# The last value block of two FFN parts: both halves joined in one step, at a higher priority

## The chip, the cores and the metric

One core of one Trainium2 chip. The metric is device time in microseconds, the median over runs. TensorE (PE in the profile) multiplies matrices into PSUM; VectorE (DVE) and ScalarE (ACT) work element by element; GpSimd (POOL) here issues the loads that add to what is already in the buffer; SyncE (SP) issues most other transfers. Each engine takes its instructions in the order that the program's scheduler wrote.

## The reference

A decoder layer over 256 tokens of width 2048. It ends with a gated FFN behind a causal convolution, and the change lies there (`h` is the residual stream):

```python
def conv_gated_ffn(hn, w_up, conv_w, conv_b, w_down):
    up = causal_dwconv(hn @ w_up, conv_w, conv_b)      # D_FF = 5632, 3 taps
    gate, val = jnp.split(up, 2, axis=-1)
    return (jax.nn.silu(gate) * val) @ w_down
...
hn = rmsnorm(h, norm_ffn_w[l])
h = h + conv_gated_ffn(hn, ffn_w_up[l], ffn_conv_w[l], ffn_conv_b[l], ffn_w_down[l])
```

Ahead of it stand two token mixers with eight wide projections and a cross-attention over 256 memory tokens. All arithmetic is float32.

## The kernel before

**Products in two pieces.** A float32 operand is split into a rounded part and the rest: `hi` and `lo` for weights (L286 on ScalarE copies `raw` into `hi`, L287 on VectorE takes `lo` = `raw` - `hi`), and one tile `s` with both pieces for activations (`split_pair`, L555 and L556). A product is then hi x hi and lo x hi (L362 and L363, in `upper_n`) and hi x lo (L369, in `lower_n`).

**The weight stream.** Weights come in pieces of 4 x 128 rows by 512 columns, 1 MB each, in one written order. `prefetch` takes the next unit of that order: it loads the piece into one of six `raw` buffers (L265 on SP; L267 on GpSimd where a piece is added onto a loaded one), and splits it into one of three `hi` and three `lo` buffers. It runs two units ahead of TensorE. Between units, `later(n, fn)` runs `fn` after n + 1 more units have been issued; this is how steps of one stage are written in among the products of the next.

**Pairs of columns.** Where two blocks of 512 columns are multiplied together (`pair_products`), eleven units replace the eight plain ones, with seven products of sums of blocks on one part of the rows. Their order and what happens to the weights:

```python
PAIR_UNITS = [
    ("q1", "A", ("new", 0, 0)), ("p0", None, (1, 8)), ("q3", "B", ("new", 1, 1)),
    ("p1", None, (0, 8)), ("q5", "A", ("add", 0, 1)), ("q2", "C", ("new", 1, 0)),
    ("q6", "A", ("sum",)), ("p2", None, (1, 12)), ("q7", "B", ("add", 0, 1)),
    ("q4", "A", ("sum",)), ("p3", None, (0, 12)),
]
```

A, B and C are `raw` buffers that stay in use. A piece is added to A for q5 and to B for q7 by the loads of L267. L294 adds B to A behind q5's split, for q6. L292 adds C to A behind q6's split, for q4. The units p0 to p3 are plain row products: p2 and p3 use the activation tiles 6 and 7, the seven q units only sums and tiles 0 to 3, p0 and p1 tiles 4 and 5. A q unit has 8 products of L362 and L363 and 4 of L369, a p unit 16 and 8. When units are done, their sums are added to the residual rows on VectorE (L427).

**The FFN.** It is cut into three parts of 4, 4 and 3 blocks of 512 hidden columns. In each part, for each block: the gate columns, then the value columns, are multiplied (`gemm_n`); the result leaves PSUM as two 16-bit planes (L757), is turned by two DMA transposes (L1205) and joined again in two halves by `join_planes` (L763 on ScalarE, two copies a half) and scaled (L1271 on VectorE). Then come the convolution (`conv`: L1281 on ScalarE, four steps of L1283 on VectorE a half), the gating and the split (`hidden`: L1354 on ScalarE, L1355 and L1356 on VectorE, then L555 and L556). The tiles that come out, two a block, are the activations of the down product, which follows as two pairs of columns in the first two parts.

`up(c0, b, at, then)` does this for one block; `at` says after how many units each half is joined. All blocks have (1, 2), the last value block of the first two parts (2, 4): its halves give tiles 6 and 7, are joined while the first pair of down columns already runs, and are first used in its eighth unit, p2. The third part has no pairs and another path there.

**What sets the order.** The program is scheduled instruction by instruction: on each engine the ready one with the lowest number goes first, and the numbers follow the order of writing. `tc.high_priority(URGENT)`, with `URGENT` 5, moves what is written inside it forward.

Of the kernel before, what the change touches and what calls it, by code (L numbers as in the profile page):

```python
# [14 lines left out]
ALU = mybir.AluOpType  # L15
# [11 lines left out]
FF = 5632  # L27
# [8 lines left out]
URGENT = 5  # L36
# [118 lines left out]
def hybrid_layer(  # L155
# [16 lines left out]
    act, dve, pe, pool, sp = nc.scalar, nc.vector, nc.tensor, nc.gpsimd, nc.sync  # L172
# [17 lines left out]
    def big(shape, dt=F32, s="b"):  # L190
        return bp.tile(shape, dt, tag="big", name=nm(s))

    def tmp(s="t"):
        return tp.tile([P, 2, S], F32, tag="tmp", name=nm(s))
# [109 lines left out]
    def later(n, fn):  # L304

        pending.append((step[0] + n + 1, fn))
# [21 lines left out]
    def gemm_t(w, row, st, nk, col):  # L328

        accs = [acc(), acc()]  # L330
        first = gemms[0] == 0
        phase = 0
        for k0, parts in chunks(nk, w, row, col):
            last = k0 + KC >= nk
            tiles = [(kk, j) for j in range(2) for kk in range(KC)]
            if first and k0 == 0:
                runs = [[(t, pr, kk, j) for t in (0, 1)] for pr in range(2) for kk in range(KC) for j in range(2)]
            elif last:
                runs = [[(t, pr, kk, j) for kk, j in tiles] for pr in range(2) for t in (1 - pr, pr)]
            else:  # L340
                runs = [[(t, pr, kk, j) for pr in range(2) for kk, j in tiles] for t in (phase, 1 - phase)]
                phase = 1 - phase
            for i, run in enumerate(runs):
                for t, pr, kk, j in run:
                    k = k0 + kk
                    sx = st[k // 2][:, k % 2, :]
                    part = parts[kk // KH][t][:, kk % KH, (2 * pr + j) * P : (2 * pr + j + 1) * P]
                    a = accs[pr][:, j, :]
                    if t == 1:
                        a, sx = a[:, S:BW], sx[:, 0:S]  # L350
                    pe.matmul(  # L351
                        a, part, sx, start=k == 0 and t == 0, stop=k == nk - 1 and t == 0, skip_group_check=True
                    )
                if i + 1 == len(runs) // 2 and not last:
                    st[(k0 + KC) // 2 + 1]
        return accs
# [14 lines left out]
    def gemm_n(w, row, st, nk, col):  # L371

        a = acc()
        for k0, parts in chunks(nk, w, row, col):
            ops = [
                [halves(st[(k0 + k) // 2], (k0 + k) % 2, slice(tt * P, (tt + 1) * P)) for k in range(KC)]
                for tt in range(2)
            ]
            for tt in range(2):
                upper_n(a[:, tt, :], ops[tt], parts, k0 == 0)  # L380
            for tt in range(2):
                lower_n(a[:, tt, :], ops[tt], parts, k0 + KC >= nk)
        return a
# [288 lines left out]
    rsb2 = rsb[:, None, :].to_broadcast([P, 2, S])  # L672

    def scaled(a, s):
        z = joined(a, s)
        dve.tensor_tensor(out=z, in0=z, in1=rsb2, op=ALU.mult)
        return z
# [72 lines left out]
    def words(t):  # L750

        return t.bitcast(U16).rearrange("p t (w two) -> p t w two", two=2)
# [6 lines left out]
    def join_planes(d, pr):  # L759

        t = tmp("jp")
        for i in range(2):
            ins = act.copy(words(t)[:, :, :, 1 - i], d[:, i, 2 * pr : 2 * pr + 2, :])  # L763
            if i == 0:
                tc.keep_in_program_order(ins)
        return t
# [115 lines left out]
    for g in range(2):  # L882
        dec = big([P, 4, S], s="dec")
        vs, turned = [], []
        for b, o in enumerate((O_Q, O_K)):
            a = qjoin if g == b == 0 else [joined(t, "q") for t in gemm_t("w_in", 0, xs, NT, o + g * BW)]
            if b == 0:
                sp.dma_start(
                    out=dec,
# [295 lines left out]
    def row_planes(o):  # L1185

        t = big([P, 2, 2, BW], U16, s="rp")
        planes(t, o)
        return t
# [11 lines left out]
    def turn_planes(rows):  # L1201

        d = big([P, 2, KC, S], U16, s="d")
        for tt in range(2):
            sp.dma_start_transpose(  # L1205
                out=d.rearrange("p a c s -> p (a c) s")[:, :, tt * P : (tt + 1) * P],
                in_=rows[:, tt].rearrange("p a w -> p (a w)"),
            )
        return d
# [51 lines left out]
    def up(c0, b, at, then):  # L1261

        if at is None:
            for pr, a in enumerate(gemm_t("ffn_w_up", 0, h2s, NT, c0 + b * BW)):
                then(pr, scaled(a, "uz"))
            return
        d = turn_planes(row_planes(gemm_n("ffn_w_up", 0, h2s, NT, c0 + b * BW)))

        def turned(pr):
            z = join_planes(d, pr)  # L1270
            dve.tensor_tensor(out=z, in0=z, in1=rsb2, op=ALU.mult)  # L1271
            then(pr, z)

        for pr in range(2):
            later(at[pr], lambda pr=pr: turned(pr))

    def conv(c0, b, pr, z, dst):
        for j in range(2):
            t = c0 // P + 4 * b + 2 * pr + j
            y = dst[:, 2 * pr + j, :]  # L1280
            act.activation(y, z[:, j, :], AF.Identity, scale=pf[:, 2, t : t + 1], bias=pf[:, 3, t : t + 1])  # L1281
            for s in range(1, 3):
                dve.scalar_tensor_tensor(  # L1283
                    out=y[:, s:S], in0=z[:, j, 0 : S - s], scalar=pf[:, 2 - s, t : t + 1], in1=y[:, s:S],
                    op0=ALU.mult, op1=ALU.add,
                )
# [55 lines left out]
    def put_rows(n, bs):  # L1342
        for b in bs:
            sp.dma_start(out=fkept[n, b], in_=hrow[b])

    def get_rows(n, bs):
        for b in bs:
            hrow[b] = big([P, 2, BW], s="nat")
            sp.dma_start(out=hrow[b], in_=fkept[n, b])

    def hidden(gt, vl, pr, summed):
        cs = slice(2 * pr, 2 * pr + 2)
        th, o = tmp("ft"), tmp("fo")
        act.activation(th, gt[:, cs, :], AF.Tanh, scale=0.5)  # L1354
        dve.scalar_tensor_tensor(out=o, in0=th, scalar=1.0, in1=gt[:, cs, :], op0=ALU.add, op1=ALU.mult)  # L1355
        dve.tensor_tensor(out=o, in0=o, in1=vl[:, cs, :], op=ALU.mult)  # L1356
        hid.append(split_pair(o, 0.5))
        if summed and len(hid_sums) < KC:
            hid_sums.append(sums(o, 0.5))
# [3 lines left out]
    for part, nb_ in enumerate(FF_PARTS):  # L1363
        final = part == len(FF_PARTS) - 1
        paired = nb_ == 4
        hid, hid_sums = [], []
        for b in range(b0, b0 + nb_):
            gt, vl = big([P, 4, S], s="fg"), big([P, 4, S], s="fv")
            last = b + 1 == b0 + nb_
            up(0, b, (1, 2), lambda pr, z, b=b, gt=gt: conv(0, b, pr, z, gt))  # L1370
            if last:
                later(0, lambda part=part, n=2 if paired else 4: get_rows(part % 2, range(n)))

            def finish_up(pr, z, b=b, gt=gt, vl=vl, paired=paired):
                conv(FF, b, pr, z, vl)
                hidden(gt, vl, pr, paired)

            up(FF, b, None if last and not paired else (2, 4) if last else (1, 2), finish_up)
        if final:
            wfin = []  # L1380
            for i in range(2):
                t = big([P, 2, BW], s="wf")
                sp.dma_start(
                    out=t.rearrange("p a n -> p (a n)"),
                    in_=final_norm_w[i * 1024 : (i + 1) * 1024].partition_broadcast(P),
                )
                wfin.append(t)
        if nb_ == 4:
            for b in (0, 2):
                if b == 0:  # L1390
                    later(8, lambda part=part: get_rows(part % 2, (2, 3)))
                pair_add("ffn_w_down", b0 * BW, hid, hid_sums, b * BW, (b + 1) * BW, hrow[b], hrow[b + 1])
                put_rows((part + 1) % 2, (b, b + 1))
        else:
            for b in range(4):
                down(b0, hid, b, final)
        b0 += nb_
# [35 lines left out]
```

## Time and profile before

| | |
|---|---|
| median of 3 runs | 1997.59 us (1996.73 to 1998.44) |
| the profiled execution | 1995.6 us, span 1993.8 us |
| instructions | 23634 |
| mean granted TensorE clock | 0.995 |
| moved by DMA | 456.59 MB, mean 229 GB/s |
| largest queue | q1: 139072 packets, 410.51 MB, 58.7% of 16 engines |

In the page's forty slices the granted clock reads 9 tenths or more in all but one (8). The first pair of down columns of part one begins near 1432 us, that of part two near 1696. In the timelines a row is start, duration, engine, line, operation, output and inputs, shapes and count, with the idle time ahead of it and what ended it in brackets. A row's duration runs a little into the next row's start: the distance from start to start is what an engine needs for one instruction in a stream.

### The profile page before, as it was taken

The numbers are of one execution on the slowest core, as the hardware profiler recorded it, in microseconds if no ns is written. First come the engines' busy times: TensorE is split into PE (matmuls) and PEld (weight loads), VectorE is DVE, ScalarE is ACT, GpSimd is POOL, SyncE is SP. The second block draws the span as 40 slices with busy tenths as digits, with TensorE's granted clock in tenths as the row PEclk, the third lists the DMA queues.
The fourth block names the chain that finished last, engine by engine and source line by source line (L and its number), as shares of the span: only waits on it lengthen the run. The fifth ranks groups of instructions, "written<-read, shape, count | busy, mean of one in ns | idle before, by whom it ended". The sixth has DMA issues, their size and how long they took to land.

```text
span 1993.8 us, 23634 instructions
## 1 busy us (share of the span) xinstructions
PE 1968.6 (99%) x9304; PEld 1650.8 (83%) x9304; DVE 1566.4 (79%) x1546; ACT 1277.2 (64%) x1323; POOL 43.2 (2%) x52
## 2 busy tenths in 40 slices
PE   9999999999999999999999999999989999899998
PEld 7888888888888888888888888888878888788887
DVE  6978888889886886779988778677786777885775
ACT  6655656767677554567778756567744667546662
POOL 0000000000000000000000000000000000000000
PEclk9999999999999999999999999999999999899999
DMA  9675674655887865878998748766777677686671
GB/s 369 233 261 147 223 264 161 230 190 160 266 260 220 248 250 190 252 256 258 270 259 235 267 125 271 236 226 204 234 232 273 207 219 236 204 278 228 211 245 61
DMA packets 146463, 456.59 MB, mean 229 GB/s; under 512 B 77744, under 2 KB 82480, under 8 KB 98608
## 3 DMA queue, kind: packets, MB, share of 16 engines
q1 hardware_dynamic: 139072, 410.51, 58.7%
q0 software_dynamic: 5760, 41.95, 11.6%
q10 hardware_dynamic: 1520, 2.63, 0.4%
q8 instruction: 73, 1.20, 0.2%
q14 instruction: 38, 0.31, 0.0%
HBM read 420.96 MB, written 16.78 MB: 220 GB/s over the span
## 4 chain that ended last, share of the span: by engine, by line
PE 91%; DVE 4%; ACT 2%; DMA 1%; issue 1%; SPq 0%; POOLq 0%; ACTq 0%; DVEq 0%
PE acc L362 25%; PE acc L363 25%; PE acc L369 24%; PE acc L351 14%; PE sm L518 2%; DVE lo L287 1%; ACT hi L286 1%; DMA raw<-in_wall 1%; PE acc L518 1%; PE sm L948 1%; PE sm L532 1%; DVE raw L294 0%; DVE fv L1283 0%; DMA d<-rp 0%; DVE tb L722 0%
## 5 line engine op out<-in xcount | busy, mean ns | idle before, releaser
L287 DVE TENSOR_TENSOR lo<-raw,hi 128x2048 fp32r<-128x2048 f32 (+1 forms) x420 | 950.9, 2267 | 297.8 <-ACT hi L286 297.0
L286 ACT CAST hi<-raw 128x2048 fp32r<-128x2048 f32 (+1 forms) x418 | 793.2, 1901 | 522.7 <-PE acc L363 374.8
L362 PE MATMUL acc<-hi,s 128*128 128x512 f32 x2008 | 787.3, 392 | 12.4 <-ACT hi L286 12.3
L363 PE MATMUL acc<-hi,s 128*128 128x512 f32 x2008 | 784.3, 391 | 0.0
L369 PE MATMUL acc<-lo,s 128*128 128x512 f32 x2008 | 501.1, 389 | 0.0
L362 PEld LDWEIGHTS acc<-hi,s 128*128 128x128 f32 x2008 | 378.6, 189 | 91.5 <-ACT hi L286 13.2
L363 PEld LDWEIGHTS acc<-hi,s 128*128 128x128 f32 x2008 | 378.9, 189 | 78.5 <-DVE s L556 1.0
L369 PEld LDWEIGHTS acc<-lo,s 128*128 128x128 f32 x2008 | 377.1, 188 | 78.3
L351 PE MATMUL acc<-s,hi 128*128 128x512 f32 x832 | 200.4, 392 | 2.1 <-DVE hi L284 1.5
L351 PEld LDWEIGHTS acc<-s,hi 128*128 128x128 f32 x832 | 153.5, 188 | 32.8 <-issue 1.6
L362 PE MATMUL acc<-hi,ss 128*128 128x512 f32 x320 | 125.8, 393 | 0.8 <-ACT o L454 0.6
L363 PE MATMUL acc<-hi,ss 128*128 128x512 f32 x320 | 124.7, 390 | 0.0
L763 ACT COPY jp<-d 128x512 uint16<-128x512 uint16 x132 | 93.4, 771 | 29.4 <-DMA d<-rp 29.3
L351 PEld LDWEIGHTS acc<-s,lo 128*128 128x128 f32 x832 | 107.1, 191 | 4.9 <-DVE lo L287 1.3
L351 PE MATMUL acc<-s,lo 128*128 128x256 f32 x832 | 110.5, 284 | 0.5 <-DVE lo L287 0.5
L369 PE MATMUL acc<-lo,ss 128*128 128x512 f32 x320 | 85.6, 389 | 0.0
L362 PEld LDWEIGHTS acc<-hi,ss 128*128 128x128 f32 x320 | 60.1, 188 | 14.5 <-ACT o L454 1.4
L369 PEld LDWEIGHTS acc<-lo,ss 128*128 128x128 f32 x320 | 60.1, 188 | 12.6
L363 PEld LDWEIGHTS acc<-hi,ss 128*128 128x128 f32 x320 | 60.1, 188 | 12.2
L267 POOL DMA_DIRECT2D raw<-in_wall x40 | 35.2, 880 | 1550.7 <-DVE lo L287 887.5
L427 DVE TENSOR_TENSOR nat<-nat,acc 128x512 f32<-128x512 f32 (+1 forms) x49 | 44.0, 910 | 14.9 <-PE acc L369 14.9
L292 DVE TENSOR_TENSOR raw<-raw,raw 128x2048 f32<-128x2048 f32 x20 | 45.8, 2288 | 0.4
(235 smaller groups left out, 1251.7 us busy)
## 6 DMA issues: line engine op xcount, KB each, us to landing
raw<-in_wall SPq DMA_DIRECT2D x333, 1024.0 KB, 5.0
raw<-in_wall POOLq DMA_DIRECT2D x40, 1024.0 KB, 8.2
fkept<-nat SPq DMA_DIRECT2D x12, 512.0 KB, 7.7
nat<-fkept SPq DMA_DIRECT2D x12, 512.0 KB, 5.6
xt<-in_x_t SPq DMA_DIRECT2D x11, 256.0 KB, 7.8
raw<-in_wall SPq DMA_DIRECT2D x5, 512.0 KB, 7.9
nat<-in_x ACTq DMA_DIRECT2D x4, 512.0 KB, 10.1
ret<-hr SPq DMA_DIRECT2D x4, 512.0 KB, 4.6
```

The source lines that it names most:

```text
L267: pool.dma_start(out=raw, in_=src, accum_op=ALU.add)
L286: act.copy(hi[:, a:b], raw[:, a:b])
L287: dve.tensor_tensor(out=lo[:, a:b], in0=raw[:, a:b], in1=hi[:, a:b].bitcast(F32), op=ALU.subtract)
L292: dve.tensor_tensor(out=to, in0=to, in1=by, op=ALU.add)
L351: pe.matmul(a, part, sx, start=k == 0 and t == 0, stop=k == nk - 1 and t == 0, skip_group_check=True)
L362: pe.matmul(o, h, hi, start=start and kk == 0, stop=False, skip_group_check=True)
L363: pe.matmul(o, l, hi, start=False, stop=False, skip_group_check=True)
L369: pe.matmul(o, h, lo, start=False, stop=stop and kk == KC - 1, skip_group_check=True)
L427: dve.tensor_tensor(out=o, in0=o, in1=i, op=op)
L518: ins = pe.matmul(o, a, b, start=start and i == 0, stop=stop and i == 2, skip_group_check=True)
L532: ins = pe.transpose(t[:, j, tt * P : (tt + 1) * P], rows[:, tt, k + j * P : k + (j + 1) * P], ident)
L763: ins = act.copy(words(t)[:, :, :, 1 - i], d[:, i, 2 * pr : 2 * pr + 2, :])
```

## The change

The last value block of the first two parts is joined with `at` (2, 2) rather than (2, 4): both halves in the same place between units, the second right behind the first. Join, scaling, convolution, gating and split of both halves are written at the higher priority. For all other blocks the new `with` has priority 0, that is none.

```diff
         def turned(pr):
-            z = join_planes(d, pr)
-            dve.tensor_tensor(out=z, in0=z, in1=rsb2, op=ALU.mult)
+            with tc.high_priority(URGENT if at[0] == at[1] else 0):
+                z = join_planes(d, pr)
+                dve.tensor_tensor(out=z, in0=z, in1=rsb2, op=ALU.mult)
             then(pr, z)
...
-            up(FF, b, None if last and not paired else (2, 4) if last else (1, 2), finish_up)
+            def finish_last(pr, z, finish_up=finish_up):
+                with tc.high_priority(URGENT):
+                    finish_up(pr, z)
+
+            if last and paired:
+                up(FF, b, (2, 2), finish_last)
+            else:
+                up(FF, b, None if last else (1, 2), finish_up)
```

`finish_up` is the convolution of the value half and `hidden`. Lines of the changed kernel behind L1270 are one higher than before, and those behind L1378 eight.

## The prediction

> **What bounds the kernel now.** I read the page first (busy shares and the chain that ended last), then TensorE's waits, then the timelines round the two places where it waits.
>
> ```profile
> span 1993.8 us, 23634 instructions
> PE 1968.6 (99%) x9304; PEld 1650.8 (83%) x9304; DVE 1566.4 (79%) x1546; ACT 1277.2 (64%) x1323; POOL 43.2 (2%) x52
> PE 91%; DVE 4%; ACT 2%; DMA 1%; issue 1%; SPq 0%; POOLq 0%; ACTq 0%; DVEq 0%
> ...
> PE acc L362 <- ACT hi L286: 12.3, 2, 6.3
> ```
>
> TensorE is busy for 99% of the span; only what it waits for can be gained. The last line, from the waits of TensorE alone, is half of its idle time: two waits, 12.3 us. The timeline puts one in each of the first two FFN parts, early in the first pair of down columns:
>
> ```profile
> 1456.66 0.39 PE L362 MATMUL acc<-hi,s 128*128 128x512 f32 x1
> 1456.88 0.39 PE L363 MATMUL acc<-hi,s 128*128 128x512 f32 x1
> ...
> 1457.34 0.39 PE L363 MATMUL acc<-hi,s 128*128 128x512 f32 x1
> 1463.79 1.33 PE L362 MATMUL acc<-hi,s 128*128 128x512 f32 x2 [6.07 <-ACT hi L286]
> ...
> 1466.23 0.63 PE L363 MATMUL acc<-hi,s 128*128 128x512 f32 x1
> 1466.66 0.63 PE L362 MATMUL acc<-hi,s 128*128 128x512 f32 x1
> ...
> 1721.53 0.39 PE L363 MATMUL acc<-hi,s 128*128 128x512 f32 x1
> 1728.19 1.33 PE L362 MATMUL acc<-hi,s 128*128 128x512 f32 x2 [6.28 <-ACT hi L286]
> ```
>
> The four products from 1456.66 are those of unit p2 with the first half of the last block. The next product in TensorE's order is q4's first, and it waits for q4's `hi`. Behind the wait a product takes 0.43 us (1466.23 to 1466.66), before it 0.22 (1456.66 to 1456.88; 0.227 over longer stretches). The granted clock tells when:
>
> ```profile
> 1461.10:1461.60 0.50, 0.00 (x0) 0.84 0.81 344
> 1468.00:1468.50 0.50, 0.50 (x3) 0.74 1.09 451
> 1723.80:1724.80 1.00, 0.00 (x0) 0.73 0.83 336
> 1734.40:1734.80 0.40, 0.40 (x3) 0.87 1.21 512
> ```
>
> The columns are the stretch, its length, TensorE's busy time, the granted clock, the DMA share and GB/s. With 1.0 and 0.5 as the only levels, the clock fell at 1461.44 and 1724.26 and rose at 1468.26 and 1734.50. These are 2 and 3 steps of 3.41 us apart, and the two falls 77 steps: the clock changes on a grid of 3.41 us. Half clock after the restart lasted 4.5 and 6.3 us and cost (0.43 - 0.227) / 0.43 = 0.47 of that, 2.1 and 3.0 us. Each place so costs some 8.7 us.
>
> **What q4's `hi` waits for.** ScalarE's and VectorE's timelines of the first place (start, duration, engine, line, and in brackets the idle time before and what ended it), and three VectorE lines of the second:
>
> ```profile
> 1441.28 0.77 ACT L763 COPY jp<-d 128x512 uint16<-128x512 uint16 x1
> 1441.91 0.62 ACT L1354 ACTIVATE ft<-fg 128x512 f32<-128x512 f32 x1
> ...
> 1452.33 0.63 ACT L555 ACTIVATE s<-fo 128x512 fp32r<-128x512 f32 x1
> 1455.34 1.92 ACT L286 CAST hi<-raw 128x2048 fp32r<-128x2048 f32 x1 [2.38 <-DMA raw<-in_wall]
> 1457.16 1.09 ACT L1281 ACTIVATE fv<-jp,pf 128x256 f32<-128x256 f32 x2
> 1461.84 1.90 ACT L286 CAST hi<-raw 128x2048 fp32r<-128x2048 f32 x1 [3.59 <-DVE raw L292]
> ...
> 1447.99 0.68 DVE L1355 SCALAR_TENSOR_TENSOR fo<-ft,fg 128x512 f32<-128x512 f32 x1
> 1448.60 2.28 DVE L287 TENSOR_TENSOR lo<-raw,hi 128x2048 fp32r<-128x2048 f32 x1
> 1450.80 0.68 DVE L1356 TENSOR_TENSOR fo<-fo,fv 128x512 f32<-128x512 f32 x1
> 1451.40 2.28 DVE L287 TENSOR_TENSOR lo<-raw,hi 128x2048 fp32r<-128x2048 f32 x1
> 1453.61 0.68 DVE L1271 TENSOR_TENSOR jp<-jp,rsb 128x512 f32<-128x512 f32 x1
> 1454.21 0.68 DVE L556 SCALAR_TENSOR_TENSOR s<-fo,s 128x512 fp32r<-128x512 f32 x1
> 1454.81 0.68 DVE L1355 SCALAR_TENSOR_TENSOR fo<-ft,fg 128x512 f32<-128x512 f32 x1
> 1455.41 2.28 DVE L287 TENSOR_TENSOR lo<-raw,hi 128x2048 fp32r<-128x2048 f32 x1
> 1457.79 1.76 DVE L1283 SCALAR_TENSOR_TENSOR fv<-jp,pf,fv 128x255 f32<-128x255 f32 x4
> 1459.47 2.28 DVE L292 TENSOR_TENSOR raw<-raw,raw 128x2048 f32<-128x2048 f32 x1
> ...
> 1712.54 0.68 DVE L1355 SCALAR_TENSOR_TENSOR fo<-ft,fg 128x512 f32<-128x512 f32 x1
> ...
> 1722.19 1.76 DVE L1283 SCALAR_TENSOR_TENSOR fv<-jp,pf,fv 128x255 f32<-128x255 f32 x4
> 1723.87 2.29 DVE L292 TENSOR_TENSOR raw<-raw,raw 128x2048 f32<-128x2048 f32 x1
> ```
>
> VectorE runs with no gap over 0.1 us from 1447.99 to the end of L292. L292 adds two weight sums; q4's `hi` is the copy of its result. It ends at 1461.75, `hi` starts 0.09 later, TensorE 1.95 after that. So TensorE's restart is set by VectorE's queue: three full splits (`lo` of q2, q6, p2; 2.20 us from start to start), five half-block steps (0.60 each), the four convolution steps of the second half (1.68), then L292.
>
> **The change, part by part.** The built order of the changed kernel differs only in these two places; at priority 0 the other joins stand where they did.
>
> VectorE. The new order from 1447.99 is: `lo` of q2, L1355, `lo` of q6, L1356 (first half), `lo` of p2, L1271 and L1355 (second half), L556 (first half), L292, and only then the four convolution steps, `lo` of q7, L1356, `lo` of q4 and L556 of the second half. The same three splits and five small steps stand ahead of L292: 3 x 2.20 + 5 x 0.60 = 9.60, so L292 starts at 1457.59 instead of 1459.47. What left is the convolution, 1.68, and the 0.2 it waited for ScalarE. Restart: 1457.59 + 2.28 + 0.09 + 1.95 = 1461.91, 1.88 earlier. Second place: 1712.54 + 9.60 = 1722.14 against 1723.87, 1.73 earlier. Sum 3.61 us.
>
> ScalarE. The second half's join is cut in two: the first half's split (L555) stands between its copies and waits for L1356, which now ends at 1453.67 rather than 1451.48. `hi` of q7 is queued behind that, but it waits for its DMA until 1455.34 anyway: 0.63 (L555), 0.77 (copy) and 0.62 (tanh) from 1453.7 end at 1455.7 at the latest, 0.4 late. `hi` of q7 and the two activations then end near 1458.7, before L292 does (1459.87): no cost. A DMA up to some 1.2 us later would now stay hidden, where before it moved L292 one for one.
>
> TensorE. One new wait: p2's second product needs L556 of the first half, now 1456.99 + 0.68 = 1457.67, and TensorE is there at 1456.88. The 0.8 us cost nothing, as the four products still end by 1458.4, long before 1461.91; if that cover went, they would be the price. After the restart the order is eight of q4, one of p2's second half, twelve of q7, the rest of p2, four of q4, p3. The second half's upper split comes after convolution (1459.79), `lo` of q7 (1461.47), L1356 (1463.67 to 1464.35) and a 0.63 copy: 1465.0. At half clock TensorE arrives at 1461.91 + 8 x 0.43 = 1465.3: no wait. At full clock it arrives at 1463.7 and waits 1.3.
>
> Queues.
>
> ```profile
> 1447.15 0.89 POOL L267 DMA_DIRECT2D raw<-in_wall  x1 [21.87 <-DVE fv L1283]
> ...
> 1438.47 23.64 SPq L265 DMA_DIRECT2D raw<-in_wall  x3
> 1462.16 0.90 SPq L1349 DMA_DIRECT2D nat<-fkept  x2
> ...
> nat<-fkept SPq DMA_DIRECT2D x12, 512.0 KB, 5.6
> ```
>
> The moved steps issue no DMA. GpSimd's adding load at 1447.15 follows L294, which stands ahead of the first difference: unmoved. On SP the last two of the three loads wait for VectorE's `lo` of p2 and L292 and go out about 1.8 us earlier. The two residual loads (L1349) now stand behind one more weight load, which waits for `lo` of q7 (near 1463.7), and so go about 2 us later. Their reader is the next pair's first add, at least 80 products x 0.227 = 18 us after the restart; they take 5.6. No cost.
>
> Clock. Both kernels fall to half clock if the shorter gap still suffices. New gap: 1458.4 to 1461.9, 3.5 us. The fall at 1724.26 came 2.3 us after the last product before it (1721.53 + 0.39), with that grid step about 0.3 busy, so 3.5 us suffices for most positions of the grid. Half clock then lasts from the restart to the end of the first full grid step, 3.4 to 6.8 us, 5.1 on average, in both kernels: no difference on average. On this profile's own grid the first place would stay at half clock until 1468.26 (6.4 instead of 4.5, 0.9 lost) and the second only until 1731.08 (4.6 instead of 6.3, 0.8 gained): 3.5 us in all.
>
> The Trainium skill (TensorE: Matmul & The Clock Gate, "What's actually happening") says that the clock falls after at least one idle window of about 3.4 us, on a window that runs freely. By it a gap of 3.5 us would hardly ever hold a whole window, and the clock would stay up. The fall 2.3 us into the gap disagrees with its letter; what it would give is rival B.
>
> Sum: 1995.6 (the profiled execution, 1.8 around its span, 2.0 below the median of the runs shown) - 3.6 = 1992.0; on the median, 1997.59 - 3.6 = 1994.0.
>
> **The rivals.**
>
> A, the forecast: the gap shrinks by 1.9 and 1.7 us and half clock stays. 1994.0; by the grid's position each place gives 0.2 to 3.4, both together mostly 2 to 5.5.
>
> B: the shorter gap no longer drops the clock. For it: 3.5 us is barely one grid step. Against: the fall after 2.3 us. Each place then gains 1.8 + 2.4 (the average price of half clock, 5.1 x 0.47) less the 1.3 us wait at full clock, 2.9: 5.8, so 1991.8.
>
> C: the earlier start is lost again behind the restart, because the second half's steps come no earlier (L556 of the second half: 1467.1 to 1467.8 in the new order, after L427 and `lo` of q4). For it: at full clock TensorE does wait there. Against: at half clock it doesn't, and q7's twelve products stand between. It would leave 0 to 1 us: about 1997.
>
> D, slower: the next pair waits. Its p0 needs an accumulator that VectorE frees with the broadcast add of q5, and that add now stands behind `lo` of p0 instead of ahead of it.
>
> ```profile
> 1471.27 1.22 DVE L427 TENSOR_TENSOR nat<-nat,acc 128x1024 f32<-128x1024 f32 x1 [3.31 <-PE acc L369]
> ```
>
> From the end of p2 VectorE needs two such adds (2.4), two splits (4.4) and a small one (0.6), 7.4; TensorE has 40 products (four of q4, p3, q1), 9.1. The slack is 1.7. If VectorE were later than this by 4.0, TensorE would stand idle for 2.3 us once more, enough by the second place to drop the clock again: 2.3 + 2.4 - 1.8 = 2.9 lost a place, 2003.4. Against: nothing in the new order adds two full splits there.
>
> **How the numbers follow.** 0.2% (4.0 us) is about what a measurement of this kernel can tell from no change. A 0.70, B 0.14, C 0.10, D 0.06. A's mean, 3.6, lies just inside 4.0; with its spread (about 1 us, the grid's position in either kernel's runs and my durations) 0.29 of its 0.70 lie beyond. Faster 0.29 + 0.14 = 0.43; same 0.41 + 0.10 = 0.51; slower 0.06. The range reaches from just beyond B (1990.8) to C's poor end (1997.6), and leaves out D and the tails.
>
> **What would show it.** Right: TensorE's two long waits shrink from 6.1 and 6.3 to about 3.5 each, with waits of 0.8 on L556 just ahead of them; L292 stands ahead of the second half's L1283 and follows L556 with no gap; half clock remains after both. Wrong: no half clock there (B); a new wait on ScalarE's L555 or VectorE's L556 behind the restart (C); a wait ahead of the next pair's p0 (D); or waits still near 6 us, which would mean that VectorE's queue didn't set the restart.

## The result and the profile after

Median 1993.55 us of 18 runs (1990.57 to 1997.76) against 1997.07 of 18 runs of the kernel before: ratio 0.9983, 95% interval 0.9976 to 0.9990, about 3.5 us faster. The forecast was 1994.0. In the changed kernel the lines behind L1270 have moved by one: the scale is L1272, the convolution L1282 and L1284, the gating L1355 to L1357.

TensorE's waits in the changed kernel (what was waited for; us in total, times, longest):

```profile
PE acc L362 <- ACT hi L286: 6.4, 2, 3.2
PE acc L363 <- DVE s L556: 2.0, 2, 1.3
PE acc L351 <- ACT hi L286: 1.7, 1, 1.7
```

The two waits for q4's `hi` fell from 12.3 us to 6.4, and a new pair of short waits, on the split of the first half, stands ahead of them. The third line is a wait 10.7 us into the kernel, ahead of anything that the change moves (0.6 us in the profiled run of before). TensorE's timeline of the changed kernel, from q1's first product to the first product of the next pair's p0, in both places:

```profile
1434.37 0.39 PE L362 MATMUL acc<-hi,s 128*128 128x512 f32 x1
...
1458.85 0.39 PE L362 MATMUL acc<-hi,s 128*128 128x512 f32 x1
1459.95 0.50 PE L363 MATMUL acc<-hi,s 128*128 128x512 f32 x1 [0.72 <-DVE s L556]
...
1464.14 0.80 PE L362 MATMUL acc<-hi,s 128*128 128x512 f32 x1 [3.22 <-ACT hi L286]
...
1484.96 0.39 PE L362 MATMUL acc<-hi,s 128*128 128x512 f32 x1
...
1697.12 0.39 PE L362 MATMUL acc<-hi,s 128*128 128x512 f32 x1
...
1723.26 0.50 PE L363 MATMUL acc<-hi,s 128*128 128x512 f32 x1 [1.28 <-DVE s L556]
...
1727.45 0.80 PE L362 MATMUL acc<-hi,s 128*128 128x512 f32 x1 [3.23 <-ACT hi L286]
...
1748.02 0.39 PE L362 MATMUL acc<-hi,s 128*128 128x512 f32 x1
```

The same four end points in TensorE's timeline of the kernel before:

```profile
1432.18 0.39 PE L362 MATMUL acc<-hi,s 128*128 128x512 f32 x1
...
1484.21 0.39 PE L362 MATMUL acc<-hi,s 128*128 128x512 f32 x1
...
1696.37 0.39 PE L362 MATMUL acc<-hi,s 128*128 128x512 f32 x1
...
1749.51 0.39 PE L362 MATMUL acc<-hi,s 128*128 128x512 f32 x1
```

Between the end points lie the same products. The first place took 52.03 us and now takes 50.59, the second 53.14 and now 50.90: 1.44 + 2.24 = 3.68 us. Between the two places (1484.21 to 1696.37, 1484.96 to 1697.12) both kernels take 212.16 us. So what the change does lies in the two places. The spans of the two profiled runs (1993.8 and 1992.7) differ by only 1.1, because the changed kernel's execution came 2.19 us later to the first place (1434.37 against 1432.18), although the program is the same up to there, and took 0.4 us more behind the second, where it has one further wait, of 0.43 us at 1931.34.

VectorE's timeline of the changed kernel shows why:

```profile
1450.20 2.29 DVE L287 TENSOR_TENSOR lo<-raw,hi 128x2048 fp32r<-128x2048 f32 x1
...
1459.21 0.69 DVE L556 SCALAR_TENSOR_TENSOR s<-fo,s 128x512 fp32r<-128x512 f32 x1
1459.81 2.29 DVE L292 TENSOR_TENSOR raw<-raw,raw 128x2048 f32<-128x2048 f32 x1
1462.02 1.66 DVE L1284 SCALAR_TENSOR_TENSOR fv<-jp,pf,fv 128x255 f32<-128x255 f32 x4
...
1469.20 0.69 DVE L556 SCALAR_TENSOR_TENSOR s<-fo,s 128x512 fp32r<-128x512 f32 x1
...
1713.51 2.28 DVE L287 TENSOR_TENSOR lo<-raw,hi 128x2048 fp32r<-128x2048 f32 x1
...
1723.13 2.28 DVE L292 TENSOR_TENSOR raw<-raw,raw 128x2048 f32<-128x2048 f32 x1
```

From `lo` of q2 to L292 it is 9.61 and 9.62 us, and the convolution (1.66) stands behind L292. ScalarE's timeline has `hi` of q7 and then `hi` of q4, which starts 0.09 us after L292 has ended (1462.10):

```profile
1457.62 1.90 ACT L286 CAST hi<-raw 128x2048 fp32r<-128x2048 f32 x1
...
1462.19 1.90 ACT L286 CAST hi<-raw 128x2048 fp32r<-128x2048 f32 x1 [1.68 <-DVE raw L292]
```

The granted clock in the changed kernel (stretch, its length, TensorE's busy time, granted clock, DMA share, GB/s):

```profile
1459.33:1462.74 3.41, 0.97 (x3) 1.00 0.72 288
1462.60:1463.60 1.00, 0.00 (x0) 0.57 0.08 33
1469.40:1470.00 0.60, 0.60 (x4) 0.85 0.97 410
1722.16:1725.58 3.42, 0.96 (x3) 1.00 0.86 307
1725.00:1726.00 1.00, 0.00 (x0) 0.79 0.59 246
1732.20:1732.60 0.40, 0.40 (x3) 0.75 1.11 471
```

The clock fell at 1462.74 and 1725.58 and rose at 1469.58 and 1732.40, so half clock was left 5.4 and 5.0 us behind the restarts. It is still there in both places.

### The profile page after: what moved, and what is told of

It is laid out like the page before. It is cut to its first block, busy times and chain, and to the rows that moved or that the text cites. A ratio compares the mean times of both kernels' runs of the same rounds, so it can differ in the third digit from the quotient of the medians.

```text
span 1992.7 us, 23630 instructions
## 1 busy us (share of the span) xinstructions
PE 1970.7 (99%) x9304; PEld 1652.7 (83%) x9304; DVE 1566.4 (79%) x1546; ACT 1277.4 (64%) x1323; POOL 43.3 (2%) x52
## 4 chain that ended last, share of the span: by engine, by line
PE 92%; DVE 3%; ACT 1%; issue 1%; DMA 1%; SPq 1%; POOLq 0%; ACTq 0%
PE acc L362 25%; PE acc L363 25%; PE acc L369 25%; PE acc L351 13%; PE sm L518 2%; DVE lo L287 1%; ACT hi L286 1%; PE acc L518 1%; PE sm L948 1%; PE sm L532 1%; DVE raw L294 0%; DMA nat<-fkept 0%; SPq L1205 0%; DMA raw<-in_wall 0%; DMA d<-rp 0%
## 5 line engine op out<-in xcount | busy, mean ns | idle before, releaser
L363 PEld LDWEIGHTS acc<-hi,ss 128*128 128x128 f32 x320 | 60.6, 189 | 12.4
L292 DVE TENSOR_TENSOR raw<-raw,raw 128x2048 f32<-128x2048 f32 x20 | 45.7, 2287 | 0.4
```

The source lines that it names most:

```text
L292: dve.tensor_tensor(out=to, in0=to, in1=by, op=ALU.add)
L363: pe.matmul(o, l, hi, start=False, stop=False, skip_group_check=True)
```

## Experiments

Two measures are used. The times are medians, each with the ratio to the kernel before run beside it; the ratio is worked out from all runs and is not the quotient of the two medians. The profiles give, for one execution, the time over the same counts of products round each place: 404 products round the first, 487 round the second. These take 100.09 and 120.01 us in the kernel before, 98.64 and 117.77 in the changed one, and they leave out what one execution loses at its start.

**Which part of the change acts.** Two kernels with one part each. In the first, both halves are joined at step 2 and every new priority is 0:

```
-            with tc.high_priority(URGENT if at[0] == at[1] else 0):
+            with tc.high_priority(0):
...
-                with tc.high_priority(URGENT):
+                with tc.high_priority(0):
                     finish_up(pr, z)
```

> Changed kernel, but every new priority set to 0: both halves joined together, nothing raised. Theory 1 (the later, common join alone moves VectorE's queue; the priority does nothing): the built order is that of the changed kernel but for the four convolution steps among themselves, so 3.5 us under the kernel before, TensorE's two waits on hi of L286 at 3.2 to 3.5 us and short waits on s of L556 (0.7 to 1.3) ahead of them. Rival (the priority does it): as the kernel before, within 1 us, the two waits at 6.1 to 6.3.

Measured: 1994.0 us, ratio 0.9983 (0.9974 to 0.9992); 98.23 and 117.55 us round the places. Its waits:

```profile
PE acc L362 <- ACT hi L286: 6.5, 2, 3.2
PE acc L363 <- DVE s L556: 1.9, 2, 1.2
```

These are the changed kernel's waits to 0.1 us. The second kernel keeps the priorities and joins the halves at steps 2 and 4:

```
-            with tc.high_priority(URGENT if at[0] == at[1] else 0):
+            with tc.high_priority(URGENT if at == (2, 4) else 0):
...
-                up(FF, b, (2, 2), finish_last)
+                up(FF, b, (2, 4), finish_last)
```

> Changed kernel with the new priorities, but the two halves joined at steps 2 and 4 as before. Theory 1 (only the common join counts): within 1 us of the kernel before, L292 behind the second half's convolution on VectorE, TensorE's two waits on hi of L286 near 6.2 us. Rival (the priority does it): 3.5 us under the kernel before, waits near 3.3.

Measured: 1997.79 us, ratio 1.0004 (0.9995 to 1.0012); 100.89 and 118.96 us. Its long waits:

```profile
PE acc L362 <- ACT hi L286: 12.7, 2, 6.6
```

So the common join gives the whole effect and the raised priority none. The blocks at priority 0 still stand in the first of these kernels; the common join without any block was not run.

**Is it the order on VectorE?** The kernel before with nothing moved but L292, in every pair of columns:

```
-                dve.tensor_tensor(out=to, in0=to, in1=by, op=ALU.add)
+                with tc.high_priority(5):
+                    dve.tensor_tensor(out=to, in0=to, in1=by, op=ALU.add)
```

> Kernel before, with one thing changed: VectorE's addition L292 is emitted at a priority raised by 5, which puts it ahead of p2's lower split (2.20) and the second half's convolution (1.68) on VectorE; the joins stay at steps 2 and 4. Theory 1 (VectorE's queue ahead of L292 sets the restart, whatever moved it): q4's wait falls from 6.2 to 2.3 to 2.6 us in both places. What is late next is the second half's split, since VectorE's work in all is the same: new waits on s of about 1.2 (ScalarE's split) and 1.9 us (VectorE's) behind the restart, so 1.0 to 1.6 us a place and 2 to 3.2 in all. Rival (the common join counts for a reason of its own, not by the order on VectorE): q4's wait stays over 5 us and the time within 1 us of before.

Measured: 1993.68 us, ratio 0.9980 (0.9971 to 0.9989); 98.83 and 117.38 us. TensorE's timeline (lines behind L292 are one higher in this kernel):

```profile
1460.63 0.50 PE L363 MATMUL acc<-hi,s 128*128 128x512 f32 x1 [2.41 <-ACT hi L286]
...
1463.62 0.79 PE L363 MATMUL acc<-hi,s 128*128 128x512 f32 x1 [0.40 <-ACT s L556]
1465.76 0.80 PE L364 MATMUL acc<-hi,s 128*128 128x512 f32 x1 [1.35 <-DVE s L557]
...
1724.74 0.68 PE L363 MATMUL acc<-hi,s 128*128 128x512 f32 x1 [3.59 <-ACT hi L286]
```

An earlier L292 alone does what the change does, without any common join. In the first place q4's wait is 2.41, as expected, and two waits on the second half's split have come behind it, 0.40 and 1.35 (expected 1.2 and 1.9). In the second place the wait is 3.59, not 2.4. ScalarE's timeline there says why:

```profile
1720.01 1.91 ACT L286 CAST hi<-raw 128x2048 fp32r<-128x2048 f32 x1 [2.45 <-DMA raw<-in_wall]
...
1722.81 1.88 ACT L286 CAST hi<-raw 128x2048 fp32r<-128x2048 f32 x1
```

The first row is `hi` of q7, held up by its load; q4's `hi` (second row) is queued behind it and has no wait of its own left. So once L292 comes early enough, the next bound is q7's load through ScalarE's queue.

**Operand in halves.** L292 and q4's `hi` in two halves each, the halves of L292 at a priority raised by 2, joins as before:

```
-            pieces = ... else ((0, 2), (2, 4)) if taken[0] <= 3 else ((0, 4),)
+            pieces = ... else ((0, 2), (2, 4)) if taken[0] <= 3 or kind == "q4" else ((0, 4),)
...
-                dve.tensor_tensor(out=to, in0=to, in1=by, op=ALU.add)
+                for h in (slice(0, 2), slice(2, 4)):
+                    with tc.high_priority(2):
+                        dve.tensor_tensor(out=to[:, h], in0=to[:, h], in1=by[:, h], op=ALU.add)
```

> Kernel before, with L292 and the copy of its result (hi of q4) in two halves each, and the halves of L292 at a priority raised by 2. The joins stay at steps 2 and 4. TensorE's gap falls into two short ones, near 1.6 us (first half of hi) and 1.7 us (second half), and a third of 1.2 us on s of L556. Theory 1 (what stands ahead of L292 on VectorE, the length of L292 and of the copy set the restart, and a gap shorter than the changed kernel's 3.2 us makes the fall of the clock rarer): 1.7 us a place less in waits, and 2.4 more where the clock stays up; 4 to 7 us in all under the kernel before. Rival on the clock (a TensorE that is idle for a third of a grid step falls to half clock all the same): half clock in both places, and 3 to 4 us in all. Rival (the waits only move behind the restart): within 1.5 us of before.

Measured: 1993.91 us, ratio 0.9979 (0.9969 to 0.9989); 97.72 and 117.64 us. TensorE's timeline of the first place (lines behind L292 two higher), and the granted clock in two steps of 3.41 us:

```profile
1459.51 0.50 PE L364 MATMUL acc<-hi,s 128*128 128x512 f32 x1 [1.60 <-ACT hi L286]
...
1462.10 0.51 PE L364 MATMUL acc<-hi,s 128*128 128x512 f32 x1 [1.37 <-ACT hi L286]
...
1464.43 0.80 PE L365 MATMUL acc<-hi,s 128*128 128x512 f32 x1 [0.89 <-DVE s L558]
```

```profile
1457.16:1460.57 3.41, 1.80 (x8) 1.00 0.00 0
1460.57:1463.98 3.41, 1.59 (x6) 1.00 0.49 168
1463.50:1464.00 0.50, 0.03 (x1) 0.96 0.97 410
```

The three waits are as expected to 0.4 us, 3.9 together in place of 6.1; in the second place they are 2.78 and 1.21, with q7's load late again. The rival on the clock was right: in the first place, with no gap over 1.6 us, it still fell, at 1463.97, behind a step in which TensorE was busy for 1.59 of 3.41 us. It had not fallen behind the step with 1.80.

**The second half one step earlier.** `(2, 4)` becomes `(2, 3)`:

> Kernel before with the second half joined one step earlier (steps 2 and 3 instead of 2 and 4), no priority. VectorE's order puts L292 at the very end, behind the second half's convolution, q7's lower split and L1356; TensorE's order does p2's second half ahead of q4. Theory 1 (the restart follows from what VectorE still has ahead of what TensorE does next, whatever that is): no long wait on hi of L286; instead about 3.1 us on ScalarE's split s of the second half and 1.9 on VectorE's, 1.2 us a place less than before, half clock in both places: 2 to 3.5 us under the kernel before. Rival (only an earlier L292 shortens the gap): the wait grows past 6.2 us and the kernel is slower than before.

Measured: 1994.35 us, ratio 0.9986 (0.9977 to 0.9995); 99.22 and 118.69 us.

```profile
PE acc L362 <- ACT s L555: 6.4, 2, 3.5
PE acc L363 <- DVE s L556: 3.0, 2, 1.6
```

No wait on q4's `hi` is left, though L292 now comes last of all: TensorE's order has p2's second half ahead of q4, and waits for that. The gain is near the others (2.2 us round the places, 3.0 by the medians). Three different orders each take 2 to 4 us off; VectorE's work as a whole is the same in all of them.

**TensorE's own order.** At the long wait of the kernel before q7's `hi` was there (1455.34 + 1.92 = 1457.26), while the built order put q4 ahead of q7. A block at priority 0 is not quite nothing: the priority counter goes back when the block ends, so what follows ties with what is inside, and neighbouring units interleave. (That a priority of 0 is none, as the section on the change says, so holds for the order built there, not in general.) First for all half units (q1 to q7) of every pair, joins at 2 and 4:

```
-                run(((o, names[kind]),), (ops,), parts)
+                with tc.high_priority(0): run(((o, names[kind]),), (ops,), parts)
```

> Kernel before; the products of the seven half units (q1 to q7) are each emitted in a block at priority 0, which resets the priority behind the block, so that the products of neighbouring units interleave on TensorE: q7's products (its hi is there by 1457.2) and p2's second half come ahead of q4's. VectorE then reaches L292 later than before, behind q7's lower split. Theory 1 (the gap is TensorE's fixed order waiting for one operand while others are there): three waits of about 0.8, 2.3 and 0.7 us in place of 6.2; 2.4 us a place less, 2.4 more where the clock stays up: 4.8 to 10 us under before. Rival on the clock (gaps of 2.3 us with work between still drop it): near 5. Rival (the blocks spoil the order in the other pairs of units): within 2 us of before or slower.

Measured: 2013.38 us, ratio 1.0070 (1.0057 to 1.0082), so for the whole kernel the rival was right. Round the two places it takes 96.41 and 114.87 us, 8.8 less than before. The same with joins at 2 and 3:

> The blocks of the kernel with levelled units and the joins at steps 2 and 3 together. Laying the built order out with the durations of the profile, TensorE has waits of about 0.9 and 1.9 us a place on the second half's splits, and none on q4's hi. Theory 1: 3.4 us a place less in waits, and half clock gone if a gap of 1.9 us is too short for it (2 to 3 us more a place): 7 to 16 us under before. Rival on the clock (1.9 us still drops it): 6 to 8. Rival (order spoilt elsewhere, or q7's load that lands 8 us after its issue becomes the wait): within 3 us of before.

Measured: 2010.06 us, ratio 1.0055 (1.0042 to 1.0069). Round the two places this kernel takes 94.44 and 113.77 us, 11.9 less than before; it comes to the first of them 23 us later (1422.9 against 1400.0). Its waits on other tiles (`o`, 0.6 us in the kernel before) are part of that:

```profile
PE acc L362 <- ACT o L454: 9.3, 6, 3.8
PE acc L362 <- ACT o L456: 4.7, 2, 3.2
```

So both were right in part: the gain is in the places, and a larger loss is elsewhere. The blocks were then put in the first pair of down columns only, joins at 2 and 3 (the lines behind are four higher):

```
-                run(((o, names[kind]),), (ops,), parts)
+                if w == "ffn_w_down" and c0 == 0:
+                    with tc.high_priority(0):
+                        run(((o, names[kind]),), (ops,), parts)
+                else:
+                    run(((o, names[kind]),), (ops,), parts)
...
-            up(FF, b, None if last and not paired else (2, 4) if last else (1, 2), finish_up)
+            up(FF, b, None if last and not paired else (2, 3) if last else (1, 2), finish_up)
```

> Kernel before, joins at steps 2 and 3, and the blocks at priority 0 around the products of the half units only in the first pair of down columns (the pair in which the two long waits lie); the order of all other pairs is that of before. Laying the built order out with the durations of the profile, TensorE has waits of 1.0 and 1.9 us a place on the second half's splits, none on q4's hi, and the next pair's p0 starts 6.1 us earlier a place if the clock then stays up. Theory 1 (the waits at the places are TensorE's and VectorE's order and nothing else; what the kernel levelled everywhere lost, it lost in the other pairs): 6 to 12 us under before, the fastest so far. Rival on the clock (a gap of 1.9 us drops it): 6 to 7. Rival (the loss lies in this pair too): not under 1995.

Measured: 1987.65 us, ratio 0.9942 (0.9930 to 0.9955), the fastest kernel of the study with the next one; 94.46 and 113.79 us. Its five runs fall into two groups, two near 1984 us, the profiled one among them, and three near 1987.7; so the gain is 9.3 us by the medians and 11.6 by the ratio. Where the three lost 3.5 us is not shown. One candidate is near 1060 us, where two of the kernels above and below (priorities alone; the common join with blocks) have a wait of 1.8 us and one step of half clock in their profiled runs, together some 3.4 us by these numbers. TensorE's waits, and the clock in the grid steps with the largest gap of each place:

```profile
PE acc L363 <- DVE s L560: 3.1, 2, 1.5
PE acc L362 <- ACT hi L286: 2.0, 2, 1.3
```

```profile
1458.55:1461.96 3.41, 1.88 (x9) 1.00 0.55 173
1461.96:1465.37 3.41, 3.41 (x17) 1.00 0.90 310
...
1717.96:1721.37 3.41, 1.87 (x8) 1.00 0.58 178
```

The `hi` in the second line is p2's (0.7 and 1.3 us), which ScalarE's order now has behind the first half's split. The clock stayed at 1.00 in both places of the profiled run (the second row is the step behind the first). The sum nearly closes: the waits went from 12.35 us to 5.1, 7.3 less, and half clock, which lasted 4.5 and 6.3 us behind the restarts before at a price of 0.47, 5.1 more; 12.4 together, 11.85 measured round the places. The rest is about what two waits more cost beside what the brackets count, some 0.3 us each (worked out below, under "3.6 us in all").

With the blocks in both pairs of down columns of a part:

> The same with the blocks in both pairs of down columns of a part. The second pair has no gating beside it. Theory 1: no wait to take away there, so the time of the kernel with the blocks in the first pair alone, within 1.5 us. Rival (interleaved products need their accumulators and weights in another order, which costs where nothing is gained): slower than that one by 2 us or more.

Measured: 1987.49 us, ratio 0.9946 (0.9932 to 0.9959): no difference. The blocks in the first pair with joins at 2 and 4, and with the changed kernel's common join:

> Kernel before (joins at steps 2 and 4) with the blocks at priority 0 around the half units' products of the first pair of down columns, nothing else. It separates the two parts of the fastest kernel so far. Theory 1 (TensorE's order is the larger part): waits of about 0.8, 2.3 and 0.7 us a place in place of 6.2. By the clock's rule as the runs show it (it fell after grid steps of 3.41 us in which TensorE was busy for 0.48 or less, and stayed after 0.53 or more), a gap of 2.3 us leaves at most 0.32 to 0.6 of a step: it falls in one place of two. 7 to 10 us under before. Rival (the join at step 3 makes the gain): within 2 us of before.

> The changed kernel (both halves joined at step 2, high priority) with the same blocks. Theory 1 (the two-halves join saves VectorE's queue ahead of L292, but with TensorE's order levelled the second half's split is what is late, and the common join makes the first half's late too): waits of about 2.0, 1.8 and 1.6 us a place, half clock in at least one place; 3 to 6 us under before, slower than the blocks with joins at 2 and 3. Rival (the gains add): 12 us or more under before.

Measured: 1988.77 us, ratio 0.9958 (0.9945 to 0.9970), 95.44 and 116.65 us, and 1993.58 us, ratio 0.9982 (0.9973 to 0.9991), 98.97 and 117.85 us. TensorE's order alone takes 8.0 us off round the places (7.75 by the medians), the larger part of the 11.85 with joins at 2 and 3. In the profiled run with joins at 2 and 4 the clock fell in the second place alone, and that place is 2.9 us behind the kernel with joins at 2 and 3. The intervals of the two ratios overlap, so this last step rests on one profile of each. The common join doesn't add to it: it makes the first half's split late too, and the gain falls back to that of the change alone. TensorE's waits in that kernel:

```profile
PE acc L362 <- ACT s L559: 5.4, 5, 2.2
PE acc L362 <- ACT hi L286: 2.8, 2, 1.5
```

**Work off VectorE.** In the changed kernel all additions L292 go to GpSimd:

```
-                dve.tensor_tensor(out=to, in0=to, in1=by, op=ALU.add)
+                pool.tensor_tensor(out=to, in0=to, in1=by, op=ALU.add)
```

> Changed kernel with all additions L292 on GpSimd instead of VectorE (every pair of columns, not only the two places). VectorE loses 2.20 us ahead of the restart, so everything of the second half comes 2.2 earlier. No row of the trace has an addition of this size on GpSimd. Theory 1 (VectorE's queue sets the restart): q4's hi is no longer tied to VectorE; if GpSimd takes no more than about 4 us and does not slow VectorE, the wait falls under 2 us and the kernel is 3 to 6 us under the changed one. Rival (GpSimd is several times slower than VectorE, or takes its access from it while both run): q4's hi comes later than 1462, waits over 3.2 us, in more pairs of columns than two, and the kernel is slower than the changed one.

Measured: 2016.57 us, ratio 1.0095 (1.0080 to 1.0111). GpSimd's and VectorE's timelines in the first place:

```profile
1469.08 11.08 POOL L292 TENSOR_TENSOR raw<-raw,raw 128x2048 f32<-128x2048 f32 x1 [5.05 <-DVE lo L287]
```

```profile
1475.73 5.90 DVE L1284 SCALAR_TENSOR_TENSOR fv<-jp,pf,fv 128x255 f32<-128x255 f32 x4
```

The addition took 11.08 us in both places (4.6 is the median of all 20), and the four convolution steps beside its end 5.90 instead of 1.66. q4's `hi` was later than ever, with waits up to 7.5 us. The rival was right that the kernel is slower; the waits over 3.2 us for q4's `hi` are in the two places alone. The loss of 19 us against the kernel before (23 against the changed one) was not taken apart: round the places it is 4.7 us (101.67 and 123.11), and the execution came to the first of them 16 us later.

## Why the prediction was right

**VectorE's queue up to L292 sets the restart.** Shown: the terms were 9.60 forecast, 9.61 and 9.62 measured; the join alone, with every priority at 0, gives all of it; and moving L292 alone, with no common join, gives as much (3.9 us round the places).

**3.6 us in all.** 3.68 round the places, 3.5 by the medians. Counted from q1's first product, TensorE restarts 29.77 us later instead of 31.61 in the first place, and 30.33 instead of 31.82 in the second: 1.84 and 1.49 us earlier, where 1.88 and 1.73 were forecast. The second is short by 0.2 because VectorE's steps there began 0.22 us later already (1713.51 - 1697.12 against 1712.54 - 1696.37), ahead of the first step that the change moves. Half clock behind the restarts lasted 5.4 us instead of 4.5, and 5.0 instead of 6.3; at the price of 0.47 that is 0.5 lost and 0.6 gained. Together 3.5 us; some 0.2 is left open. That half clock nearly cancels is where the grid lay in these two executions: the forecast had no difference on average, and that its sum came out so close is luck in that part.

The brackets say a little more than the restarts: from 6.07 and 6.28 to 0.72 + 3.22 and 1.28 + 3.23 they are 3.9 us less together. A bracket counts from the end of a product, 0.39 us behind its start, where the next would have started after 0.23; and the first product behind a wait takes 0.11 longer (1459.95 to 1460.29 is 0.34). So each of the two new waits costs some 0.3 us that no bracket shows.

**The waits of the second product of p2.** 0.8 forecast, 0.72 and 1.28 measured; they were hidden as said, since TensorE had to wait for q4 anyway.

**The side paths.** `hi` of q7 was forecast up to 0.4 late and came 0.1 late in the first place (23.25 us behind q1's first product instead of 23.16) and 0.4 late in the second (23.81 instead of 23.37); the residual loads went out 2.0 and 2.3 us later, where 2 was forecast. Neither cost anything: no wait of TensorE follows in either place.

**Half clock remains (rival B falls).** Right, and its length was near: 5.4 and 5.0 us behind the restarts, where this profile's grid gave 6.4 and 4.6 and the average 5.1. The Trainium skill (TensorE: Matmul & The Clock Gate, "What's actually happening") lets the clock fall after at least one idle window of about 3.4 us. Here it fell behind steps with 0.97 and 0.96 us of work, so the traces disagree if idle means without any work: a step that is busy for less than about half is enough to lose it. By the shares listed at the end rival B needs the grid to cut the gap near its middle, so its chance was smaller than the 0.14 given.

**Nothing behind the restart (rivals C and D fall).** Neither place has a wait between q4's restart and the next pair's p0. The second half's L556 ended 35.5 us behind q1's first product (1469.20 + 0.69 - 1434.37), where rival C's figures gave 35.6, and at half clock that was in time. The experiments show how near C was: an L292 that is 4.1 us earlier than before, instead of 1.8, meets waits of 0.40 and 1.35 there.

**What the prediction did not see.** It took TensorE's order as given. The 6 us wait was for one unit, while the next one in the order could have run; that order alone was worth twice what the change gave round the places (8.0 us against 3.7), and with the second half joined one step earlier three times (11.85).

## What to carry over

When an in-order engine waits long for one operand, list first what else it could have done at that moment: here putting other ready work there took 8.0 us off round the two places, hurrying the operand 3.7 to 4.7. But only there: the same blocks in all pairs of columns made the kernel 13 to 16 us slower. Hurrying it pays only down to the next item of the same queue, since the feeding engine's work in all stays the same. And where a gap also costs the clock, find the gap that is short enough not to. In the second place of the two kernels with blocks in the first pair, 0.7 us less of waits (2.81 for 3.52) went with 2.9 us less in all (joins at 2 and 3 for 2 and 4, one profile of each).

## What was not expected of the hardware

**The clock follows the busy share of a fixed step.** Round the two places the clock fell at the end of a 3.41 us step of a fixed grid: the two falls lie 77 steps apart both before and after (1461.44 and 1724.26, 1462.74 and 1725.58). TensorE's busy share of the step ahead of a fall was 0.48 or less (0.00 and 0.31 before, 0.28 and 0.28 after, 0.48, 0.34, 0.42, 0.47, 0.40 in experiments); behind steps with 0.53 (two of them) and 0.55 (two) it stayed. So the limit is near half, and it isn't sharp: elsewhere in the kernel with levelled units and joins at 2 and 3 the clock stayed behind a step with 0.46 (1.56 of 3.41 us, from 1105.48). By these shares a gap of up to some 1.5 us costs only itself (an estimate: 1.9 of 3.41 us are then left busy, 0.56), and two short ones in one step can cost the clock.

**GpSimd beside VectorE.** An addition of 128x2048 took GpSimd 4.6 us in the median of 20, twice VectorE's 2.28, and 11.08 in the two places, where VectorE had no pause; the splits beside it kept their 2.28. The Trainium skill (GPSIMD Engine Reference, "1. Specifications") has the two share their access to the memory, with contention where an instruction of VectorE takes two inputs from it. The traces agree in part: 11.08 and 5.90 us where 4.6 and 1.66 were to be expected, but the splits take two inputs as well and paid nothing. What decides who pays, no run here shows.
